# Value products of a sparse attention in one burst, compressed values last, probability tiles copied back in place

## The chip, the cores and the metric

One core of a Trainium2 chip runs the program. The time is that of the device, in microseconds, as the median of three runs. Below, PE is TensorE's matmul stream, PEld its weight loads, DVE is VectorE, ACT ScalarE, POOL GpSimd.

## What is computed

The reference is two layers of a decoder trunk over 512 tokens of width 1024. A layer's mixer sums three gated branches; the change touches one of them, the sparse attention with 8 heads in 2 groups (head width 64). For each query it adds three attentions over the same query, each weighted by a gate:

```
p_cmp = masked_softmax(s_cmp, cmp_mask)            # 31 compressed blocks of 32 tokens
o_cmp = einsum('bghsn,bngd->bsghd', p_cmp, vc)
...                                                 # selected blocks: all 8 of 64 tokens are taken at this length
p = masked_softmax(s, mask);  o_sel = einsum('bgqhn,bgqnd->bgqhd', p, vg)
...                                                 # window of 512 tokens: all earlier tokens
o_win = einsum('bnghqk,bnkgd->bnqghd', p_win, vw)
g = sigmoid(gate_logits)
o = g[..., 0:1] * o_cmp + g[..., 1:2] * o_sel + g[..., 2:3] * o_win
```

The other branches are two chunked linear recurrences. After the mixer come a cross attention over 256 memory tokens and a gated MLP with a short convolution.

## The kernel before

**Dense work.** Activations stand transposed (features on partitions, 512 tokens in a row). A weight arrives by DMA in pieces of 128 x 512, is split into a rounded part (ACT, into `wh`) and a rest (DVE, into `wl`), and each 128 x 128 piece is then used in three matmuls of 512 columns into one of three PSUM banks of the tag `pd`. There are three buffers for arriving weights and two for converted ones. Such dense matmuls (`fm_scaled` for the gates, `branch` for the branches' output weights) stand in the program before and after `nsa_attn`.

**The attention, `nsa_attn` (from line 1027).** The outer loop goes over four query blocks i of 128 tokens. Each makes the compressed scores and their probabilities for all heads, gated, transposed, in `pc`. The inner loop goes over four values of j, each a pair of heads, one of each group g_; this text calls such a pair a head. There are 16 heads per layer and 32 in all. For a head and each of 2 groups x 2 branches (br 0 selected, 1 window):

1. score matmuls (L1080 to L1082, 128 x (i+1) keys, into a `pa` bank), the maximum on DVE (L1084), the exponential on ACT into a tile `pr` of the tag `chain`, with its sum;
2. when all four are there: reciprocal, gate, and a scaling of the four `pr` (DVE, L250);
3. transposes of each `pr` in pieces of 128 (L1100, into a `pt` bank), and a copy of the bank by ACT into a new `chain` tile `pT`;
4. an output bank `po` of the tag `pa`: the compressed values (`vcpad`) times `pc` open the accumulation, two matmuls; then for each branch, each key block k and each group a value product `tok` x `pT`. Group 0 writes partitions 0 to 63, group 1 partitions 64 to 127;
5. a copy of the bank into the output `y` by ACT.

One fp32 product of step 4 shows as two instructions in the trace, so the compressed pair is x4 and the value products of a head in block i are x8(i+1). Transposes are x4(i+1).

**Buffers.** `chain` has 36 buffers, `pa` two banks, `pt` three.

**What sets the order.** The program's text gives each engine no fixed order. A planner goes through the instructions at build time, places on each engine what it takes to be ready, earliest in the program first (weight conversions ahead by a raised priority), gives out buffers as they come free, and sets a semaphore wait for each dependence on another engine. On the chip each engine's matmuls or operations then run in the order so fixed. Dense matmuls that stand in the program after the attention are thereby placed between its steps where these are not ready.

Of the kernel before, what the change touches and what calls it, by code (L numbers as in the profile page):

```python
# [13 lines left out]
AF = mybir.ActivationFunctionType  # L14
# [5 lines left out]
P = 128  # L20
# [179 lines left out]
def tile_trunk(ctx, tc, a, out, dbg=None):  # L200
    nc = tc.nc
    dbg = dbg or {}
    V, S, G, TE = nc.vector, nc.scalar, nc.gpsimd, nc.tensor
# [7 lines left out]
    def tl(tag, bufs, shape=(P, T), dt=F32):  # L211
        uid[0] += 1
        return sb.tile(list(shape), dt, tag=tag, name=f"{tag}_{uid[0]}", bufs=bufs)

    def chain():
        return tl("chain", NCHAIN)
# [5 lines left out]
    def pa():  # L222
        uid[0] += 1
        return pp.tile([P, T], F32, tag="pa", name=f"pa_{uid[0]}", bufs=2)

    def pt():
        uid[0] += 1
        return pp.tile([P, T], F32, tag="pt", name=f"pt_{uid[0]}", bufs=3)

    def small(n, dt=F32):  # L230
        if n <= 16:
            return tl("tiny", 40, (P, 16), dt)[:, :n]
        return tl("small", 10, (P, 64), dt)[:, :n]

    def mm(out_, lhsT, rhs, start=True, stop=True):
        TE.matmul(out_, lhsT, rhs, start=start, stop=stop, skip_group_check=True)  # L236
# [5 lines left out]
    def act(o, i, f=AF.Copy, **kw):  # L242
        S.activation(o, i, f, **kw)  # L243

    def tt(o, x, y, op, eng=None):
        (eng or V).tensor_tensor(o, x, y, op)  # L246

    def ts(o, x, s1, s2, op0, op1=None, eng=None):
        if op1 is None:
            (eng or V).tensor_scalar(o, x, s1, None, op0)  # L250
        else:
            (eng or V).tensor_scalar(o, x, s1, s2, op0, op1)
# [6 lines left out]
    def mark(name):  # L259
        if "mark" in dbg:  # L260
            dbg["mark"](name, nc)
# [193 lines left out]
    vcpad = [cst.tile([P, 4, 64], F32, name=f"vcpad{i}") for i in range(2)]  # L455
# [571 lines left out]
    def nsa_attn(l, tok, y, st):  # L1027
        KH, KL, QS, kcT, r8 = (st[k] for k in ("KH", "KL", "QS", "kcT", "r8"))
        mark("attn")
        gall = tl("gall", 1, (P, NT, 24))  # L1030
        act(gall, tok[:, :, TOK_G:TOK_G + 24], AF.Tanh, scale=0.5)
        ts(gall, gall, 0.5, 0.5, MUL, ADD)

        for i in range(NT):
            qs_ = slice(i * P, (i + 1) * P)
            sc = pa()
            for j in range(4):
                for g_ in range(2):
                    mm(sc[:, (4 * g_ + j) * 64:(4 * g_ + j + 1) * 64], QS[j, g_][:, qs_],
                       kcT[:, g_].rearrange("p a n -> p (a n)"))  # L1040
            e = tl("tg", NTG)[:, :256].rearrange("p (h n) -> p h n", h=8)
            m3 = cmpm[:, i:i + 1, :].to_broadcast([P, 8, 32])
            pen = tl("cmpn", 1, (P, 32))
            ts(pen, cmpm[:, i, :], -NEG, NEG, MUL, ADD)
            p3 = pen[:, None, :].to_broadcast([P, 8, 32])
            s4 = sc.rearrange("p (h a n) -> p h a n", a=2, n=32)
            tt(e, s4[:, :, 0], p3, ADD)
            tt(e, e, s4[:, :, 1], ADD)
            b8 = lambda t_, n_=32: t_.rearrange("p (h o) -> p h o", o=1).to_broadcast([P, 8, n_])
            tt(e, e, b8(r8[:, i]), MUL)  # L1050
            mx = small(8)
            V.tensor_reduce(mx, e, AX.X, MAX)
            tt(e, e, b8(mx), SUB)
            act(e, e, AF.Exp)
            tt(e, e, m3, MUL)
            dn = small(8)
            V.tensor_reduce(dn, e, AX.X, ADD)
            ts(dn, dn, 1e-30, None, MAX)
            V.reciprocal(dn, dn)
            g3 = gall[:, i, :].rearrange("p (h b) -> p h b", b=3)  # L1060
            cf = small(8)
            tt(cf, dn, g3[:, :, 0], MUL)
            tt(e, e, b8(cf), MUL)
            ps = pt()
            for g_ in range(2):
                TE.transpose(ps[:, g_ * P:(g_ + 1) * P], e[:, g_ * 4:g_ * 4 + 4, :].rearrange("p h n -> p (h n)"), ident)
            pc = tl("tg", NTG)
            act(pc[:, :256], ps[:, :256])

            for j in range(4):  # L1070
                hd = {}
                W = (i + 1) * P
                WM = max(W, 256)
                den = small(4)
                prs = []
                for g_ in range(2):
                    for br in range(2):
                        q_ = QS[j, g_][:, qs_]
                        ps = pa()
                        mm(ps[:, :WM], q_, KH[br, g_][:, :WM], stop=False)  # L1080
                        mm(ps[:, :WM], q_, KL[br, g_][:, :WM], start=False, stop=False)
                        mm(ps[:, i * P:W], identb, negb, start=False, stop=True)  # L1082
                        nm = small(1)
                        V.tensor_reduce(nm, ps[:, :W], AX.X, MAX, negate=True)  # L1084
                        rc = r8[:, i, 4 * g_ + j:4 * g_ + j + 1]
                        tt(nm, nm, rc, MUL)
                        pr = chain()
                        act(pr[:, :W], ps[:, :W], AF.Exp, bias=nm, scale=rc, accum_out=den[:, 2 * g_ + br:2 * g_ + br + 1])
                        prs.append(pr)
                V.reciprocal(den, den)  # L1090
                g4 = gall[:, i, :].rearrange("p (g j b) -> p g j b", g=2, b=3)[:, :, j, 1:]
                tt(den.rearrange("p (g b) -> p g b", g=2), den.rearrange("p (g b) -> p g b", g=2), g4, MUL)
                for g_ in range(2):
                    for br in range(2):
                        x_ = 2 * g_ + br
                        pr = prs[x_]
                        ts(pr[:, :W], pr[:, :W], den[:, x_:x_ + 1], None, MUL)
                        pst = pt()
                        for k in range(i + 1):
                            TE.transpose(pst[:, k * P:(k + 1) * P], pr[:, k * P:(k + 1) * P], ident)  # L1100
                        pT = chain()
                        act(pT[:, :W], pst[:, :W])
                        hd[g_, br] = pT
                po = pa()
                o_ = [po[g_ * 64:(g_ + 1) * 64, :P] for g_ in range(2)]
                for g_ in range(2):
                    mm(o_[g_], vcpad[g_][:, j, :], pc[:, g_ * P:(g_ + 1) * P], start=True, stop=False)
                for br, off in ((0, TOK_VS), (1, TOK_VW)):
                    for k in range(i + 1):
                        for g_ in range(2):  # L1110
                            mm(o_[g_], tok[:, k, off + g_ * 64:off + g_ * 64 + 64], hd[g_, br][:, k * P:(k + 1) * P],
                               start=False, stop=(br == 1 and k == i))
                act(y[j][:, qs_], po[:, :P])
                yield

# [92 lines left out]
    def mixer(l, norm):  # L1208
# [68 lines left out]
        for _ in nsa_attn(l, tok, ya, st):  # L1277
            pass
# [169 lines left out]
```

## Time and profile before

| | us |
|---|---|
| median of 3 runs | 2110.43 (2110.14 to 2110.9) |
| span of the profiled execution | 2108.7 |
| TensorE busy (matmuls) | 2057.5 |
| TensorE busy (weight loads) | 1610.2 |
| VectorE busy | 1430.0 |
| ScalarE busy | 951.3 |
| GpSimd busy | 131.9 |

The profiled execution's own time is its span and what lies around it before the first and after the last instruction; only the span is in the profile. Busy times are read against it. Matmuls overlap in the pipeline and their ends are modelled, so the distance from one start to the next tells what a matmul costs the stream, and its own duration doesn't. The two attention stretches are 372 to 554 us (layer 0) and 1405 to 1588 us (layer 1) from the span's start.

### The profile page before, as it was taken

What the parts mean: (1) busy time and instruction counts of PE and PEld (TensorE: products, weight loads), DVE (VectorE), ACT (ScalarE), POOL (GpSimd) and SP (SyncE); (2) the same over time, 40 slices, a digit from 0 to 9 for tenths busy, and PEclk for the clock granted to TensorE, in tenths of its full rate; (3) what the DMA queues carried; (4) which work ended last, traced back from release to release, by engine and by line L of the source; (5) the groups of instructions that cost most, each with busy time, mean ns of one, the idle gap of its engine ahead of it and who ended that gap; (6) DMA issues with size and microseconds to landing.
All of it is one profiled execution on the core that took longest, in us unless ns stands there. A gap on an engine that the chain in (4) does not pass through costs nothing. (4 is left out here: it accounts for less than half of the span.)

```text
span 2108.7 us, 31046 instructions
## 1 busy us (share of the span) xinstructions
PE 2057.5 (98%) x11396; PEld 1610.2 (76%) x11400; DVE 1430.0 (68%) x3070; ACT 951.3 (45%) x1854; POOL 131.9 (6%) x120
## 2 busy tenths in 40 slices
PE   8999999999999999999999998999999999999999
PEld 7877677777786788888888776777778758888887
DVE  6764898666656887377548469975667577755773
ACT  6434444555545544244434344445554454433442
POOL 1000122000010100000000003110000110000000
PEclk9999999999999999999999999999999999999999
DMA  7332222111241233323432312121113413333333
GB/s 237 90 101 68 77 74 64 52 51 46 64 140 47 88 95 95 95 94 96 120 107 76 101 42 90 59 72 51 46 46 91 126 52 92 95 93 98 95 98 108
DMA packets 116809, 180.90 MB, mean 86 GB/s; under 512 B 19696, under 2 KB 37232, under 8 KB 116656
## 3 DMA queue, kind: packets, MB, share of 16 engines
q1 hardware_dynamic: 88992, 158.64, 25.1%
q10 hardware_dynamic: 27584, 19.97, 3.3%
q8 instruction: 90, 1.47, 0.3%
q14 instruction: 63, 0.52, 0.1%
q0 software_dynamic: 80, 0.29, 0.0%
HBM read 170.21 MB, written 8.65 MB: 85 GB/s over the span
## 5 line engine op out<-in xcount | busy, mean ns | idle before, releaser
L236 PE MATMUL pd<-act,wh 128*128 128x512 f32 x3008 | 985.4, 403 | 0.0
L243 ACT ACTIVATE wh<-wr 128x512 fp32r<-128x512 f32 (+2 forms) x586 | 365.5, 624 | 657.5 <-PE pd L236 566.3
L236 PEld LDWEIGHTS pd<-act,wh 128*128 128x128 f32 x3008 | 560.6, 189 | 128.4 <-issue 14.4
L236 PE MATMUL pd<-act,wl 128*128 128x512 f32 x1504 | 605.6, 403 | 1.4 <-DVE wl L246 1.4
L246 DVE TENSOR_TENSOR wl<-wr,wh 128x512 fp32r<-128x512 f32 (+2 forms) x586 | 406.7, 694 | 212.3 <-ACT wh L243 205.0
L236 PE MATMUL pd<-chain,wh 128*128 128x512 f32 x1344 | 426.7, 397 | 4.4 <-DVE gate L255 3.2
L236 PEld LDWEIGHTS pd<-act,wl 128*128 128x128 f32 x1504 | 284.3, 189 | 69.0 <-issue 6.1
L236 PEld LDWEIGHTS pd<-chain,wh 128*128 128x128 f32 x1344 | 251.0, 188 | 66.0 <-ACT chain L243 3.7
L236 PE MATMUL pd<-chain,wl 128*128 128x512 f32 x672 | 266.4, 396 | 0.3
L246 DVE TENSOR_TENSOR gate<-pd,rb 128x512 f32<-128x512 f32 x168 | 116.0, 691 | 102.8 <-PE pd L236 101.3
L236 PE MATMUL pa<-chain,chain 128*64 128x64 f32 (+7 forms) x1248 | 163.2, 296 | 2.3 <-ACT chain L243 1.0
L236 PEld LDWEIGHTS pd<-chain,wl 128*128 128x128 f32 x672 | 126.6, 188 | 30.3 <-DVE wl L246 1.1
L255 DVE SCALAR_TENSOR_TENSOR gate<-gate,vec,gate 128x511 f32<-128x511 f32 (+1 forms) x176 | 132.1, 751 | 21.5 <-ACT gate L243 18.3
L236 PEld LDWEIGHTS pa<-chain,chain 128*64 128x64 f32 (+3 forms) x1248 | 109.1, 163 | 45.5 <-issue 21.0
L1084 DVE TENSOR_REDUCE tiny<-pa 128x1 f32<-128x128 f32 (+3 forms) x128 | 61.1, 487 | 81.7 <-PE pa L236 81.3
L243 ACT ACTIVATE chain<-pa,tiny,r 128x128 f32<-128x128 f32 (+3 forms) x128 | 78.9, 617 | 60.7 <-DVE tiny L246 56.3
L246 POOL TENSOR_TENSOR chain<-chain,t 128x512 f32<-128x512 f32 x30 | 40.7, 1355 | 1014.7 <-ACT t L243 949.0
L243 ACT ACTIVATE chain<-pt 128x512 f32<-128x512 f32 (+3 forms) x156 | 61.1, 445 | 63.9 <-PE pt L1100 37.2
L243 ACT ACTIVATE gate<-gate,vec 128x512 f32<-128x512 f32 x88 | 63.8, 726 | 27.9 <-DVE gate L246 27.9
L236 PE MATMUL pa<-chain,tok 128*64 128x128 f32 x704 | 62.3, 282 | 0.0
L255 DVE SCALAR_TENSOR_TENSOR t<-t,gate 128x512 f32<-128x512 f32 x88 | 60.5, 688 | 2.0 <-ACT t L243 0.4
L246 POOL TENSOR_TENSOR tg<-tg,chain 128x256 f32<-128x256 f32 (+1 forms) x42 | 45.5, 1089 | 191.1 <-ACT tg L243 78.5
(238 smaller groups left out, 2001.5 us busy)
## 6 DMA issues: line engine op xcount, KB each, us to landing
wr<-in_w_fm SPq DMA_DIRECT2D x184, 256.0 KB, 2.7
wr<-in_w_up SPq DMA_DIRECT2D x176, 256.0 KB, 2.6
wr<-in_w_dn SPq DMA_DIRECT2D x64, 256.0 KB, 2.7
wr<-in_w_mix SPq DMA_DIRECT2D x32, 256.0 KB, 2.7
wr<-in_w_dn SPq DMA_DIRECT2D x32, 192.0 KB, 2.4
wr<-in_w_tk SPq DMA_DIRECT2D x16, 272.0 KB, 2.9
wr<-in_w_kv SPq DMA_DIRECT2D x16, 256.0 KB, 3.8
chain<-in_cmp_w SPq DMA_DIRECT2D x16, 256.0 KB, 4.1
```

Source lines behind the costliest of these rows:

```text
L236: TE.matmul(out_, lhsT, rhs, start=start, stop=stop, skip_group_check=True)
L243: S.activation(o, i, f, **kw)
L246: (eng or V).tensor_tensor(o, x, y, op)
L255: V.scalar_tensor_tensor(o, x, s, y, op0, op1)
L1084: V.tensor_reduce(nm, ps[:, :W], AX.X, MAX, negate=True)
```

## The change

The copy out of the transposes' bank goes back into `pr` and not into a new tile. The first value product of each group (br 0, k 0) gets, besides its own dependences, one on the head's last copy, and opens the accumulation. The compressed products come last and close it. Nothing else in the program differs.

```diff
                         for k in range(i + 1):
                             TE.transpose(pst[:, k * P:(k + 1) * P], pr[:, k * P:(k + 1) * P], ident)
-                        pT = chain()
-                        act(pT[:, :W], pst[:, :W])
-                        hd[g_, br] = pT
+                        copied = S.activation(pr[:, :W], pst[:, :W], AF.Copy)
+                        hd[g_, br] = pr
                 po = pa()
                 o_ = [po[g_ * 64:(g_ + 1) * 64, :P] for g_ in range(2)]
-                for g_ in range(2):
-                    mm(o_[g_], vcpad[g_][:, j, :], pc[:, g_ * P:(g_ + 1) * P], start=True, stop=False)
                 for br, off in ((0, TOK_VS), (1, TOK_VW)):
                     for k in range(i + 1):
                         for g_ in range(2):
-                            mm(o_[g_], tok[:, k, off + g_ * 64:off + g_ * 64 + 64], hd[g_, br][:, k * P:(k + 1) * P],
-                               start=False, stop=(br == 1 and k == i))
+                            m_ = TE.matmul(o_[g_], tok[:, k, off + g_ * 64:off + g_ * 64 + 64],
+                                           hd[g_, br][:, k * P:(k + 1) * P],
+                                           start=(br == 0 and k == 0), stop=False, skip_group_check=True)
+                            if br == 0 and k == 0:
+                                tc.add_manual_dep(m_.ins, copied.ins.name, mybir.DependencyInfo(
+                                    mybir.DependencyClass.Sync, mybir.DependencyReason.DATA), reason="one burst")
+                for g_ in range(2):
+                    mm(o_[g_], vcpad[g_][:, j, :], pc[:, g_ * P:(g_ + 1) * P], start=False, stop=True)
                 act(y[j][:, qs_], po[:, :P])
```

## Rows read from the trace of the kernel before

**Rows 1.** The page, first part: busy us of each engine, share, instructions.
```profile
PE 2057.5 (98%) x11396; PEld 1610.2 (76%) x11400; DVE 1430.0 (68%) x3070; ACT 951.3 (45%) x1854; POOL 131.9 (6%) x120
```

**Rows 2.** Stretches: us, busy (count) of PE, PEld, DVE, ACT, POOL; clock, DMA, GB/s.
```profile
372.00:554.00 182.00, 182.00 (x1153) 133.83 (x1152) 112.72 (x326) 101.06 (x265) 0.00 (x0) 1.00 0.16 47
1405.00:1588.00 183.00, 182.93 (x1154) 134.02 (x1152) 113.25 (x327) 101.45 (x266) 0.00 (x0) 1.00 0.16 47
```

**Rows 3.** Waits: engine, line, waited for; us in total, times, longest.
```profile
PEld pa L236 <- issue: 52.0, 167, 3.1
```

**Rows 4.** Groups on PE, 372 to 554: count, busy us, mean ns, idle before.
```profile
L236 PE MATMUL pa<-chain,tok 128*64 128x128 f32 x320 | 27.2, 280 | 0.0
...
L236 PE MATMUL pa<-tg,vcpad 128*64 128x128 f32 x64 | 7.0, 298 | 0.0
```

**Rows 5.** Timeline of PE, first head of block 2: start, us, operation, count.
```profile
454.52 0.47 PE L236 MATMUL pd<-act,wl 128*128 128x512 f32 x1
454.92 0.44 PE L236 MATMUL pa<-tg,vcpad 128*64 128x128 f32 x4
455.29 0.72 PE L236 MATMUL pd<-chain,wh 128*128 128x512 f32 x2
455.85 0.62 PE L236 MATMUL pd<-act,wh 128*128 128x512 f32 x2
456.31 0.39 PE L236 MATMUL pd<-chain,wl 128*128 128x512 f32 x1
...
459.03 0.43 PE L236 MATMUL pa<-chain,tok 128*64 128x128 f32 x2
459.39 0.50 PE L236 MATMUL pd<-act,wh 128*128 128x512 f32 x1
459.82 1.52 PE L236 MATMUL pa<-chain,tok 128*64 128x128 f32 x22
461.28 0.62 PE L236 MATMUL pa<-chain,chain 128*128 128x384 f32 x2
461.74 0.23 PE L236 MATMUL pa<-negb,identb 128*128 128x128 bf16 x1
```

**Rows 6.** Timeline of PE: last head of block 1, and the next scores.
```profile
445.25 1.09 PE L236 MATMUL pa<-chain,tok 128*64 128x128 f32 x14
446.27 0.62 PE L236 MATMUL pa<-chain,chain 128*128 128x384 f32 x2
```

**Rows 7.** Timeline of PE: first product of the first and the last broken head.
```profile
393.75 0.43 PE L236 MATMUL pa<-chain,tok 128*64 128x128 f32 x2
...
1545.20 0.43 PE L236 MATMUL pa<-chain,tok 128*64 128x128 f32 x2
```

**Rows 8.** Timeline of ACT for the head of rows 5: probability copies, output copy.
```profile
458.01 1.64 ACT L243 ACTIVATE chain<-pt 128x384 f32<-128x384 f32 x4 [1.65 <-PE pt L1100]
...
461.38 0.28 ACT L243 ACTIVATE chain<-pa 128x128 f32<-128x128 f32 x1 [1.09 <-PE pa L236]
```

**Rows 9.** Timelines: the first head of block 0, the second of block 3.
```profile
378.32 0.95 ACT L243 ACTIVATE chain<-pt 128x128 f32<-128x128 f32 x4
378.89 0.87 PE L236 MATMUL pa<-chain,tok 128*64 128x128 f32 x8
379.69 0.50 PE L236 MATMUL pd<-act,wl 128*128 128x512 f32 x1
...
524.83 2.06 ACT L243 ACTIVATE chain<-pt 128x512 f32<-128x512 f32 x4 [2.68 <-PE pt L1100]
526.07 2.35 PE L236 MATMUL pa<-chain,tok 128*64 128x128 f32 x32
528.35 0.73 PE L236 MATMUL pa<-chain,chain 128*128 128x512 f32 x2
```

**Rows 10.** Timeline behind layer 0's attention: last output split, first branch product.
```profile
555.87 0.68 DVE L246 TENSOR_TENSOR chain<-chain,chain 128x512 fp32r<-128x512 f32 x1
...
560.00 0.62 PE L236 MATMUL pd<-chain,wh 128*128 128x512 f32 x2
```

## The prediction

> **What bounds the kernel now.** I read the page first, then the stretches, the waits, the groups and last the order on TensorE. TensorE is busy for 2057.5 of 2108.7 us, VectorE for 68% [rows 1]. In the two stretches in which the attention runs, TensorE is busy all the time at a granted clock of 1.00, that is the 2.4 GHz level, while ScalarE and VectorE are busy for 55 and 62% [rows 2]. So only work or lost slots on TensorE can shorten these stretches, or work that runs out beside them.
>
> The Trainium skill (Perfetto Trace Analysis, "Identifying the Most-Contended Engine") warns that matmul busy time is a bad measure of what is left, since matmuls are pipelined; the next row bears that out. The weight loads ahead of matmuls into `pa` stand idle for 52.0 us in 167 places, and no other engine is named [rows 3]: the array is between two kinds of matmul. The value products (320 in one stretch) and the compressed products (64) use 64 columns of the array, the dense ones all 128 [rows 4].
>
> **What a break costs** is read from starts in TensorE's order, in the first head of the third query block [rows 5]. Dense matmuls follow each other every 0.23 us (two from 455.85 to 456.31). Ahead of the compressed products a dense one takes 454.52 to 454.92 = 0.40, and the products take 0.37 until the next dense one: 0.77, of which 0.23 is the dense matmul's own. So this little group costs 0.54 us. Later the value products come in two pieces: one product (x2) takes 0.36, a single dense one 0.43 (0.20 over its own), the other eleven (x22) 1.46 until the next scores. A run of x14 takes 1.02 [rows 6]; eight instructions more, two pairs of both head groups, cost 0.44, so a pair inside a run takes 0.22. The compressed pair stands 0.37, so leaving a run costs 0.15, and the lone product 0.36 - 0.15 = 0.21, as much as a pair: it has no partner in the other half of the array.
>
> **The change, part by part.**
> 1. Compressed products last. Per head 0.54 goes and one more pair at the end of the burst, 0.22, comes: 0.32 x 32 heads = **10.2 us**. The output copy by ScalarE follows that pair, and next to nothing else waits for it. No DMA is issued by what moves, and no queue but TensorE's is passed.
> 2. One burst. A product in two pieces costs 0.36 + 0.43 - 0.23 + 1.46 = 2.02 us; six pairs and one exit cost 6 x 0.22 + 0.15 = 1.47. Gain 0.55 per broken head. Through both stretches 20 of the 32 heads are broken (the first and the last in [rows 7]), 18 times by one dense matmul, else by transposes: 20 x 0.55 = **11.0 us**.
> 3. The added wait. The first products wait for the fourth copy, not the first. In the head of [rows 5] the copies end at 458.01 + 1.64 = 459.65, 0.62 us after the products began [rows 8]. In a first block it is 0.38 (379.27 against 378.89), in a last block 0.82 (526.89 against 526.07) [rows 9]; the second block is put between, at 0.50 (an estimate from its neighbours). All heads: 8 x (0.38 + 0.50 + 0.62 + 0.82) = 18.6 us. Queued behind the waiting matmul are TensorE's own: the rest of the burst, the next scores, dense matmuls. In a broken head a dense matmul was ready to stand in the gap, so I take the wait as covered there by dense matmuls drawn forward, which have to be run anyway. Going from transposes to a dense one and then into the burst (0.20) replaces going from transposes straight into it, which I put at zero, within 0.2 either way. In the 12 unbroken heads (four of the first block, two of the second, six of the last) nothing ready stood between; uncovered it is 4 x 0.38 + 2 x 0.50 + 6 x 0.82 = 7.4 us. Against that, these heads wait inside the burst now: x32 should take 8 x 0.22 + 0.15 = 1.91 and takes 2.28 (528.35 - 526.07), x8 should take 0.59 and takes 0.80 (379.69 - 378.89). This goes: 6 x 0.37 + 4 x 0.2, and 2 x 0.2 with the second block taken like the first, = 3.4. Net between -3.4 (covered) and +4.0 us; I take **+1**, a little on the uncovered side: the x32 head, the longest of these waits, found no dense matmul before, though a longer gap leaves it more time to.
> 4. Copies in place. The four ScalarE copies stay as long (1.64 us for four), and read the same transposes they waited for already. Four of the 36 `chain` buffers per head are not taken. The waits view names none for a free buffer, so I count 0. A gain is not excluded (to -2, an allowance without a row); a loss I exclude, since a head now takes four buffers where it took eight.
> 5. The output bank. Now one of two `pa` banks is taken at 454.92 by the compressed products and freed by the output copy at 461.38 + 0.28 = 461.66 [rows 5, 8]: 6.7 us. Then its first writer comes after the copies, at 459.65. If the planner hands out the bank only with that first write, the next head's scores get it nearly 5 us sooner and heads overlap more; if it keeps it from the turn of the output tile in the program, nothing changes. The trace before can't tell. TensorE has no idle time to win there, so I count 0 in the sum, but it decides the rivals.
>
> Sum: -10.2 - 11.0 + 1 = -20.2 us. The profiled span is 2108.7; the median of the runs is 2110.4, 1.7 us more, which lies around the span and stays. 2110.4 - 20.2 = **2090 us**.
>
> The Trainium skill (TensorE: Matmul & The Clock Gate, "Part 3: Packing small matmuls") says that a weight load overlaps running matmuls only where its row group differs. Both halves here use all rows, so by that page a product gains nothing from a partner. The two lone ones of a broken head (the first, and the one left over of eleven) would then cost no more than in pairs, part 2 would lose one slot of 0.22 per broken head, 20 x 0.22 = 4.4 us, and the time would be 2094. The row of x22 against x14 shows a pair in 0.22 where one alone takes 0.21, so the trace does not agree, and the sum stays.
>
> **Rivals.**
> - *Heads overlap more.* With the bank free early, scores run ahead, every wait for the copies is covered (another 4.4 us) and the pairs of scores that queue just behind a burst (0.46 from 461.28 to 461.74 [rows 5], where two of 384 columns at the dense 0.23 per 512 would take 0.35) lose some 0.1 us each, in 32 heads to twice as often. 2090 - 4.4 - 5 (of 3 to 6) = 2081. For it: the bank is held 6.7 us, a burst needs it for 2. Against: the scores may need VectorE and ScalarE first.
> - *The attention's own chain sets the stretch.* If the bank is kept, a head's chain (scores, exponential, transposes, copies, burst, output copy, next scores) ends where the burst ends. By the row sums the new end is 459.65 + 7 x 0.22 + 0.15 = 461.34 against 461.28, but in an unbroken last-block head 526.89 + 9 x 0.22 + 0.15 = 529.02 against 528.35, +0.67. Summed with the other blocks in the same way the chain grows some 4 to 6 us a layer, while TensorE's work falls by 10. The dense work beside the attention is nearly used up at its end: the last split of its output ends at 555.87 + 0.68 = 556.55, and the branch product that needs it starts at 560.00 [rows 10], so 3.4 us are left, and matmuls of the branch that don't need the last output can run ahead: with two buffers of converted weights, nine of twelve matmuls each, 18 x 0.23 = 4.2 us more. Then the gain is 3.4 to 7.6 minus 5 per layer, from +1.6 lost to 2.6 gained: 2105 to 2113, no change.
> - *Slower: the last copy comes late.* In that same case a weight conversion (0.63 us on ScalarE, taken ahead by its priority) lands between the copies. If half the heads get one, the chain grows by 16 x 0.63 = 10 and 5 us more per layer; less 3.4 to 7.6 of cover that is 7 to 12 us per layer: about 2125 to 2134. It decides from a growth of some 0.34 us per head (the mean cover of 5.5 us over 16 heads). For it: all waits become one, at the head of an in-order queue. Against: four copies now run within 1.64 us unbroken [rows 8].
> - *Only half of it happens.* Dense matmuls of higher priority still break the burst, and only part 1 pays, 2100. The dependence makes all products ready at once, which speaks against it.
>
> **How the numbers follow.** The forecast (2084 to 2095) 0.50; half of it (2095 to 2105) 0.20; more overlap (below 2084) 0.13; the chain sets the stretch (2105 to 2113) 0.10; slower 0.07. Outside 0.2%, or 4.2 us, which is about what a measurement of this kernel can tell from no change, lies all of the first three and a part of the fourth: faster 0.84, same 0.09, slower 0.07. To hold 8 in 10 the range takes the first two whole, the overlap case down to 2079 (its 2081 and the 2 us of part 4) and the fourth to 2107: 2079 to 2107.
>
> **What would show it.** Right: in TensorE's order no compressed products ahead of the transposes, one run of value products per head with the compressed pair at its end, the idle time of weight loads before `pa` matmuls down by some 15 us or more, dense matmuls between transposes and burst. The x22 row becomes x24 without a break. The two stretches should each be about 10 us shorter with TensorE still busy throughout. Wrong: TensorE idle before the burst with ScalarE named, or idle after the last head ahead of the branch products (the chain); or bursts in pieces (half of it). The planner orders the whole program anew, so other stretches may move by a few us, which I have no row for; if they move by 10, the forecast fails for a reason outside these steps.

## The result, and the profile after

The changed kernel takes 2137.26 us (2135.89 to 2141.9, four runs) against 2110.28 in runs of the kernel before beside it: ratio 1.0132 [1.0119, 1.0144]. It is **slower by 27 us**, where 20 us less was forecast.

First the busy times, which answer to [rows 1].

```profile
PE 2050.4 (96%) x11396; PEld 1614.0 (76%) x11400; DVE 1433.6 (67%) x3070; ACT 957.4 (45%) x1854; POOL 133.2 (6%) x120
```

The span is 2136.5 us. TensorE was idle for 2108.7 - 2057.5 = 51.2 us before and for 2136.5 - 2050.4 = 86.1 us now: 34.9 more, while its busy time fell by 7.1; 34.9 - 7.1 = 27.8 is the longer span. Where the idle time lies is read from windows. The rows have the columns of [rows 2].

```profile
456.00:512.00 56.00, 56.00 (x364) 43.09 (x363) 38.07 (x95) 29.76 (x70) 0.00 (x0) 1.00 0.19 59
512.00:528.00 16.00, 15.61 (x79) 11.58 (x76) 12.53 (x33) 7.69 (x17) 0.00 (x0) 1.00 0.16 50
528.00:576.00 48.00, 34.28 (x251) 26.79 (x249) 19.37 (x50) 22.56 (x49) 0.00 (x0) 0.82 0.05 12
1560.00:1624.00 64.00, 44.81 (x312) 34.40 (x306) 31.09 (x79) 29.76 (x63) 0.00 (x0) 0.89 0.06 17
```

Up to 528 us the attention of layer 0 shows TensorE busy (but for 0.4 us) at a clock of 1.00, as before [rows 2]. Then 13.7 of 48 us are idle and the clock falls; in the second layer 19.2 of 64. In the kernel before the same two windows have 0.2 us of idle time each:

```profile
528.00:576.00 48.00, 47.77 (x275) 36.89 (x272) 32.03 (x64) 24.30 (x49) 0.00 (x0) 1.00 0.22 61
1560.00:1624.00 64.00, 63.77 (x362) 50.17 (x361) 43.90 (x81) 32.44 (x63) 0.00 (x0) 1.00 0.22 67
```

So 32.4 of the 34.9 us lie in these two windows, at the **end of each layer's attention**, and not in the blocks ahead of it, whose heads have the edit's wait as well. The next view is the dense matmuls (tile `pd`) of the changed kernel alone: us, busy (count), clock.

```profile
512.00:530.00 18.00, 13.66 (x50) 1.00 0.19 59
530.00:576.00 46.00, 2.42 (x8) 0.81 0.03 6
```

The dense work beside the attention is used up at 530 us, and the attention goes on nearly alone until its last value product at 575.33; before, that product stood at 552.36, with dense matmuls beside it to the end. So the attention ends 23 us later and has lost its cover. Why it became longer is seen where TensorE still is busy: the second head of block 2, in TensorE's order (the columns of [rows 5]).

```profile
473.81 0.62 PE L236 MATMUL pa<-chain,chain 128*128 128x384 f32 x2
...
474.31 0.59 PE L236 MATMUL pa<-chain,chain 128*128 128x384 f32 x2
...
476.71 0.54 PE L236 MATMUL pa<-chain,chain 128*128 128x384 f32 x2
...
478.84 0.61 PE L236 MATMUL pa<-chain,chain 128*128 128x384 f32 x2
...
482.67 0.49 PE L1100 MATMUL pt<-cm,chain 128*128 128x128 f32 x3
...
484.15 1.14 PE L1100 MATMUL pt<-cm,chain 128*128 128x128 f32 x9
...
485.98 1.53 PE L1108 MATMUL pa<-chain,tok 128*64 128x128 f32 x24
487.34 0.39 PE L236 MATMUL pa<-tg,vcpad 128*64 128x128 f32 x4
487.66 0.61 PE L236 MATMUL pa<-chain,chain 128*128 128x384 f32 x2
```

The burst is what was wanted: twelve products without a break in 487.34 - 485.98 = 1.36 us, the compressed pair behind them in 0.32. But all four score groups of a head stand **behind the burst** of the head ahead of it (473.81 to 478.84), and none of the next head's comes before its transposes and burst are through (487.66). In the kernel before, one group ran ahead. The same head there; the burst and the score group right behind it, at 461.28, are in [rows 5]:

```profile
456.77 0.51 PE L236 MATMUL pa<-chain,chain 128*128 128x384 f32 x2
...
461.78 0.60 PE L236 MATMUL pa<-chain,chain 128*128 128x384 f32 x2
...
464.20 0.51 PE L236 MATMUL pa<-chain,chain 128*128 128x384 f32 x2
...
465.47 0.44 PE L236 MATMUL pa<-tg,vcpad 128*64 128x128 f32 x4
...
468.03 0.51 PE L236 MATMUL pa<-chain,chain 128*128 128x384 f32 x2
...
469.66 0.49 PE L1100 MATMUL pt<-cm,chain 128*128 128x128 f32 x3
```

Only three groups of this head follow the burst (461.28, 461.78, 464.20); a fourth had been there ahead of it, at 456.77. The compressed products take the output's bank at 465.47, and a score group of the *next* head stands at 468.03, ahead of the transposes. So its maximum and exponential pass while the head ahead of it is still being transposed.

**The theory.** The two `pa` banks are given to the tiles in the order of the program. The output tile `po` stands there ahead of the next head's scores. Before, its first writer (the compressed products) needs nothing of this head, so it claims its bank at once, and the tile behind it, the next scores, gets the other. After, its first writer waits for the last copy, so the claim comes late, and **the tiles behind it wait too, though a bank is free**. The head loses its overlap, the attention grows, its cover of dense work ends too soon. The planner's hand-out itself is in no trace, but what it leaves on the chip is. In the changed kernel's second head of block 2, ScalarE reads the last of the four score groups out of its bank until 480.78 + 0.67 = 481.45:

```profile
480.78 0.67 ACT L243 ACTIVATE chain<-pa,tiny,r 128x384 f32<-128x384 f32 x1 [0.83 <-DVE tiny L246]
```

The burst writes its bank from 485.98 on. For the 4.5 us between, TensorE's order has no matmul into either `pa` bank. Dense matmuls and this head's transposes fill that time; the next head's scores, which need nothing of this head, don't stand there. In all 32 heads of the changed kernel the order is four score groups, transposes, burst, compressed pair. In the kernel before, a score group of the next head stands between compressed products and transposes in 24 heads, all but the last of each block; there, in six of eight, it is the next block's compressed scores.

The rivals: the added wait itself, the copies in place, or a cost on TensorE of the new accumulation order.

### The profile page after: what moved, and what is told of

It reads as the page before. It is cut to its first block, busy times and chain, and to the rows that moved or that the text cites. A ratio compares the mean times of both kernels' runs of the same rounds, so it can differ in the third digit from the quotient of the medians.

```text
span 2136.5 us, 31148 instructions
## 1 busy us (share of the span) xinstructions
PE 2050.4 (96%) x11396; PEld 1614.0 (76%) x11400; DVE 1433.6 (67%) x3070; ACT 957.4 (45%) x1854; POOL 133.2 (6%) x120
## 4 chain that ended last, share of the span: by engine, by line
PE 85%; DVE 9%; ACT 2%; issue 2%; DMA 1%; DVEq 0%; ACTq 0%; POOLq 0%
PE pd L236 67%; PE pa L236 11%; PE pt L1100 2%; PE pa L1108 2%; DVE wl L246 2%; DVE chain L246 2%; DVE gate L246 1%; ACT chain L243 1%; DVE tg L246 1%; PE pt L236 1%; DMA wr<-in_w_kv 1%; PE pt L430 1%; DVE gate L255 0%; DVE tiny L1084 0%; DVE act L255 0%
## 5 line engine op out<-in xcount | busy, mean ns | idle before, releaser
L255 DVE SCALAR_TENSOR_TENSOR gate<-gate,vec,gate 128x511 f32<-128x511 f32 (+1 forms) x176 | 132.1, 751 | 21.3 <-ACT gate L243 18.2
L1100 PE MATMUL pt<-cm,chain 128*128 128x128 f32 x320 | 58.4, 327 | 14.6 <-DVE chain L250 14.4
L1101 ACT ACTIVATE chain<-pt 128x128 f32<-128x128 f32 (+3 forms) x128 | 51.0, 437 | 43.2 <-PE pt L1100 27.9
L1100 PEld LDWEIGHTS pt<-cm,chain 128*128 128x128 f32 x320 | 46.4, 169 | 28.2 <-DVE chain L250 21.8
```

Of the source, the lines that this page charges most:

```text
L255: V.scalar_tensor_tensor(o, x, s, y, op0, op1)
L1101: copied = S.activation(pr[:, :W], pst[:, :W], AF.Copy)
```

## The experiments

**e1_in_place.** The kernel before, with the copies in place alone.

```diff
-                        pT = chain()
-                        act(pT[:, :W], pst[:, :W])
-                        hd[g_, br] = pT
+                        act(pr[:, :W], pst[:, :W])
+                        hd[g_, br] = pr
```

> The kernel before with one part of the change alone: the probability copy goes back into its own tile. Three theories of the 27 us. Bank: the pa banks are handed out in the order of the program, and the output tile, whose first matmul now stands behind the copies, holds up the next head's first scores. Wait: the burst's wait for the last copy lengthens each head. In place: the probability tiles are held longer, through the burst. Bank and wait: no change, 2107 to 2114 us. In place: most of the loss, 2125 to 2137.

2108.56 us against 2110.61, ratio 0.9994 [0.9983, 1.0005]: nothing. The copies neither cost nor bring a measurable time; 22 of the 32 heads are still in pieces (20 before).

**e2_first_and_burst.** The change, with the compressed products back at the front; the added wait stays.

```diff
+                for g_ in range(2):
+                    mm(o_[g_], vcpad[g_][:, j, :], pc[:, g_ * P:(g_ + 1) * P], start=True, stop=False)
...
-                                           start=(br == 0 and k == 0), stop=False, skip_group_check=True)
+                                           start=False, stop=(br == 1 and k == i), skip_group_check=True)
...
-                for g_ in range(2):
-                    mm(o_[g_], vcpad[g_][:, j, :], pc[:, g_ * P:(g_ + 1) * P], start=False, stop=True)
```

> The changed kernel with the compressed products back in front, opening the accumulation; the value products still wait for the last copy, copies still in place. Bank: the output's bank is claimed early again, one score group of the next head runs ahead of the transposes, 11 us of the burst are saved and the chain grows by the wait alone: 2098 to 2112 us, TensorE idle in the last block only a little. Wait: still slow, 2125 to 2140. In place: still slow, 2125 to 2140.

2095.97 us, ratio 0.9928 [0.9910, 0.9946]: 14.6 us faster than before. The wait for the last copy is in this kernel and costs it nothing that shows, so it isn't the cause of the loss. In its order a score group stands ahead of the transposes again:

```profile
455.91 0.44 PE L236 MATMUL pa<-tg,vcpad 128*64 128x128 f32 x4
...
456.84 0.51 PE L236 MATMUL pa<-chain,chain 128*128 128x384 f32 x2
...
459.17 1.62 PE L1100 MATMUL pt<-cm,chain 128*128 128x128 f32 x12
...
461.42 1.53 PE L1110 MATMUL pa<-chain,tok 128*64 128x128 f32 x24
```

**e3_last_no_wait.** The change without the added dependence.

```diff
-                            if br == 0 and k == 0:
-                                tc.add_manual_dep(m_.ins, copied.ins.name, mybir.DependencyInfo(
-                                    mybir.DependencyClass.Sync, mybir.DependencyReason.DATA), reason="one burst")
```

> The changed kernel without the added dependence: compressed products last, copies in place, each value product waits only for its own copy. Bank: the output's bank is claimed by the first value product, still behind the transposes, so no score runs ahead: slow, 2120 to 2137 us, with TensorE idle in the last block of each layer. Wait: the compressed products' 10 us are gained, 2098 to 2106. In place: 2125 to 2140.

2134.5 us, ratio 1.0112 [1.0088, 1.0137]. Without the wait the loss is still there: compressed products last are enough for it. The first products now wait for the first copy instead of the last, which still is late. In many heads a score matmul of the next head stands right behind that first product, which fits the theory: it comes as soon as the output has claimed its bank.

```profile
481.60 0.43 PE L1108 MATMUL pa<-chain,tok 128*64 128x128 f32 x2
481.96 0.44 PE L236 MATMUL pa<-chain,chain 128*128 128x384 f32 x1
482.34 1.42 PE L1108 MATMUL pa<-chain,tok 128*64 128x128 f32 x21
```

**e4_own_bank and e4b_before_own_bank.** The output tile gets a bank of its own (the transposes give one up); the first in the changed kernel, the second in the kernel before, so that the price of the banks is known by itself.

```diff
-        return pp.tile([P, T], F32, tag="pt", name=f"pt_{uid[0]}", bufs=3)
+        return pp.tile([P, T], F32, tag="pt", name=f"pt_{uid[0]}", bufs=2)
...
-                po = pa()
+                uid[0] += 1
+                po = pp.tile([P, T], F32, tag="po", name=f"po_{uid[0]}", bufs=1)
```

> The changed kernel with a PSUM bank of its own for the attention's output, taken from the transposes (two in place of three); everything else as in the change. Bank: the next heads' scores run ahead of the transposes by two or three groups, TensorE no longer idle in the last block, the 21 us of the burst come through less what the missing transpose bank costs: 2085 to 2103 us. Wait or in place: still slow, 2125 to 2140.

> The kernel before with the output bank of its own (two transpose banks, not three), and nothing of the change. It tells how much of the 25.7 us that the changed kernel with its own bank gained is the bank's and how much the change's. If the change's TensorE savings (10 from the compressed products, 11 from the burst) come through only now: 2102 to 2112 us here. If the bank alone makes the gain: 2085 to 2095.

e4: 2084.86 us, ratio 0.9881 [0.9863, 0.9899]. e4b: 2117.66 us, ratio 1.0040 [1.0028, 1.0053]. The new banks alone cost 7 to 9 us; with them the change is worth 2117.66 - 2084.86 = 33 us. Nothing but the banks was altered in e4, so, with e2, the late claim in a *shared* set of banks carries the loss; no extra cost of the accumulation order on TensorE is left.

**e5_scores_ahead.** The two shared banks as in the change, but the next head's first score group is written into the program ahead of the output tile, inside a block. For that the score group became a function, `score`; only the lines that call it ahead are shown.

```diff
...
+                if j < 3:
+                    den_ = small(4)
+                    ahead = den_, [score(j + 1, 0, den_)]
                 po = pa()
```

> The changed kernel, with the next head's first score group written in the program ahead of the output tile (within a block; not from one block to the next). PSUM banks as in the change. Hand-out in the order of the program: the first scores get their bank before the output tile stands in line, heads overlap by one group as before the change, and the savings come through: 2088 to 2106 us. If the bank were held, or two banks too few for the burst, whatever the order in the program: 2125 to 2140.

2138.15 us, ratio 1.0138 [1.0123, 1.0153]: a **miss**, 2088 to 2106 had been expected. The place of a head's last value product in layer 0, us from the span's start, tells how far it came:

| us | before | after | e5 |
|---|---|---|---|
| last head of block 1 | 446.07 | 455.18 | 447.23 |
| first head of block 2 | 461.07 | 473.39 | 467.97 |
| last head of block 2 | 496.92 | 511.72 | 505.00 |
| first head of block 3 | 514.26 | 531.80 | 528.14 |
| last head of block 3 | 552.36 | 575.33 | 576.04 |

Inside the first blocks most of the loss is taken back. But at the change of block, where the old order was left, e5 falls behind: 447.23 to 467.97 is 20.7 us against 15.0 before, and 505.00 to 528.14 is 23.1 against 17.3. In the kernel before, the next block's compressed scores, whose tile is of the tag `pa` too, ran ahead there (those of block 2 from 442.05, four us before the last product of block 1). In e5, as in after, they stand behind the last head's burst (those of block 3 from 505.42). With 13.9 us lost by 528 us e5 also meets the end of the dense work, and there it loses what it was ahead of after:

```profile
505.00:528.10 23.10, 23.10 (x145) 17.87 (x143) 16.09 (x39) 11.23 (x24) 0.00 (x0) 1.00 0.19 58
528.10:576.00 47.90, 32.51 (x201) 25.28 (x199) 17.54 (x46) 19.82 (x42) 0.00 (x0) 0.68 0.02 6
```

TensorE is idle for 15.4 of the last 47.9 us, at a clock of 0.68 where after has 0.82: more of its work is done at half the clock. Why its crossings take 2.5 and 3.1 us more than those of after (18.2 and 20.1) stays open.

**e7_ahead_across.** e5, and at the last head of a block the next block's compressed scores and first score group are written ahead of the output tile as well. Banks as in the change. The diff is against e5; the compressed scores became a function, `compressed`.

```diff
...
-                if j < 3:
+                n_ = 4 * i + j + 1
+                if n_ < 4 * NT:
+                    if n_ % 4 == 0:
+                        pcs[n_ // 4] = compressed(n_ // 4)
                     den_ = small(4)
-                    ahead = den_, [score(j + 1, 0, den_)]
+                    ahead = den_, [score(n_ // 4, n_ % 4, 0, den_)]
```

> As the run with the first scores written ahead of the output tile, and the same from block to block: the next block's compressed scores and its first score group also stand in the program ahead of the last head's output tile. That run kept the heads' distance of before within a block (13.2, 11.6, 12.3 us in block 2) and lost it between blocks (17 to 23 us against 15 to 17). If the hand-out in program order is the cause, the distances between blocks return as well: 2090 to 2108 us, TensorE not idle in the last block by more than 2 us per layer. If something else in the change lengthens the chain: 2120 to 2138.

2089.13 us, ratio 0.9904 [0.9888, 0.9921]. The order of the tiles alone takes back 48 us from after. The crossings into blocks 2 and 3 now take 13.8 and 14.3 us, and the layer's last value product stands at 549.61. Its order in block 2, and the window to the end of layer 0's attention:

```profile
458.33 1.53 PE L1124 MATMUL pa<-chain,tok 128*64 128x128 f32 x24
459.69 0.39 PE L236 MATMUL pa<-tg,vcpad 128*64 128x128 f32 x4
460.01 0.62 PE L236 MATMUL pa<-chain,chain 128*128 128x384 f32 x2
...
460.51 0.59 PE L236 MATMUL pa<-chain,chain 128*128 128x384 f32 x2
...
463.38 0.58 PE L236 MATMUL pa<-chain,chain 128*128 128x384 f32 x2
...
464.16 0.51 PE L236 MATMUL pa<-chain,chain 128*128 128x384 f32 x2
...
467.18 0.49 PE L1110 MATMUL pt<-cm,chain 128*128 128x128 f32 x3
```

```profile
498.00:550.00 52.00, 51.80 (x362) 38.79 (x360) 33.14 (x78) 30.68 (x66) 0.00 (x0) 1.00 0.17 52
```

Three of the four groups behind the burst belong to this head, the fourth (464.16) to the next one. TensorE is busy to the end at full clock.

**e6_more_cover and e6b_before_more_cover.** Is it the lost cover that makes the longer chain cost time? Both kernels get 72 dense matmuls per layer behind the attention whose result nobody reads.

```diff
+        for n in range(3):
+            fm_proj(norm, w_fm(l, f"mb{n}"))
```

> The changed kernel with 72 dense matmuls more per layer, put behind the attention in the program, whose results nothing reads: at 0.23 us each 16.7 us per layer, 33.4 in all. If the loss is dense work that ran out beside a longer chain of heads, these fall into the idle and half-clock time of the last block: 2135 to 2150 us, hardly slower than the changed kernel (2137). If the time was lost otherwise: 2165 to 2172.

> The kernel before with the same 72 dense matmuls more per layer, as the price of the addition where TensorE is not idle: 2110 + 33 = 2140 to 2148 us by either theory.

In the kernel before the extra work costs 38 us (2146.63 against 2108.82, ratio 1.0177 [1.0153, 1.0200]). In the changed one it costs nothing: 2134.72 (1.012 [1.010, 1.014]) against 2137.26 without. So the time at the attention's end was empty enough to take it whole, and with this cover in both the change is 2146.63 - 2134.72 = 12 us *faster* than the kernel before. The window of after's idle time, in the changed kernel with this cover:

```profile
528.00:576.00 48.00, 43.93 (x311) 33.12 (x311) 26.23 (x60) 25.13 (x54) 0.00 (x0) 0.93 0.14 39
```

It is not filled whole (43.93 of 48 us, clock 0.93), which fits 12 us and not the 20 forecast.

**e8_own_bank_no_wait.** e4 without the added dependence (the diff of e3): what the burst is worth once the bank is out of the way.

> The changed kernel with an output bank of its own, without the added dependence on the last copy. With the chain out of the way it prices the burst alone: value products are in pieces again, and if these cost what the rows of before said (0.55 us for each of some 20 broken heads) the time is some 8 to 12 us more than the 2084.9 of the run with the dependence: 2092 to 2098 us. If the wait costs as much as the burst saves: 2082 to 2088.

2105.05 us, ratio 0.9971 [0.9962, 0.9980]: the burst is worth 2105.05 - 2084.86 = 20.2 us. Other work stands between the products in 28 of the 32 heads, in none of e4's. One of these:

```profile
463.69 0.43 PE L1109 MATMUL po<-chain,tok 128*64 128x128 f32 x2
464.06 0.50 PE L236 MATMUL pd<-act,wh 128*128 128x512 f32 x1
464.39 0.33 PE L236 MATMUL pa<-chain,chain 128*128 128x384 f32 x1
464.66 1.42 PE L1109 MATMUL po<-chain,tok 128*64 128x128 f32 x21
```

The prediction's price of 0.55 us a head gives 28 x 0.55 = 15.4 us; here two visitors stand in the gap, and some heads are in three pieces.

## Why the prediction was wrong, point by point

1. **Compressed products last (10.2 us).** On TensorE as forecast: the group's 0.54 us ahead of the transposes are gone, the pair at the burst's end takes 487.66 - 487.34 = 0.32 where 0.22 + 0.15 = 0.37 was put for it with the exit. No run does this part alone in the two shared banks. With a bank of its own for the output, e8 against e4b does it (the copies in place, which e1 priced at nothing, differ too): 2117.66 - 2105.05 = 12.6 us. In the shared banks e7 is 6.8 us faster than e2, which lacks it, but the two also differ in order.
2. **One burst (11.0 us).** Right in kind: none of 32 heads is broken. In size it was too low: e8 against e4 gives 20.2 us for 28 heads, 0.72 each where 0.55 was put. One dense matmul alone stands in the gap of 16 of the 20 heads, not 18; in the other four (401.38 and 494.55 in layer 0, 1434.79 and 1527.95 in layer 1) there are transposes as well, and two of the 16 have a second gap with transposes in it. The weight loads' idle time ahead of `pa` was to fall by 15 us or more. The row of [rows 3] falls from 52.0 to 40.2, but the value products now have a row of their own, in which ScalarE is named:

```profile
PEld pa L236 <- issue: 40.2, 136, 3.1
...
PEld pa L1108 <- ACT chain L1101: 15.3, 32, 1.1
```

   ScalarE's name ahead of the burst was to be a sign of being wrong, yet e7, which gains, has such a row too (11.7 us, 32 times). This sign did not tell the two cases apart. Parts 2 to 4 were put at -10; e2, which does these three, gave -14.6. The size was somewhat low.
3. **The added wait (+1).** Right that it is covered while dense work lasts: e2 keeps it and gains, e3 drops it and is still slow. Where the dense work has run out, TensorE does stand idle for it, 0.69 us in the head at 543.79 (the last view below).
4. **Copies in place (0).** Right (e1).
5. **The output bank (0).** *This step failed.* It named two outcomes: the bank is handed out with its first write and the next scores get it sooner, or it is kept from the turn of the tile in the program and nothing changes. The runs show a third one: handed out late, and until then no later tile of the tag gets any bank. The account of the planner ahead of the prediction, by which buffers are given out as they come free, lacks this order. I looked at how long *one* bank is held, and not at who stands in line behind the claim. That the moved products open a claim that had cost nothing was to be seen in [rows 5]: they stand 459.03 - 454.92 = 4.1 us ahead of the first value product. A score group of the next head stands between, at 456.77, in the part that I left out of those rows.
6. **The rival with the chain** named the right place ("idle after the last head ahead of branch products") and the right point of decision, the dense work that is left, but its growth was mis-sized: 4 to 6 us a layer, from the burst's end alone. The last value product of layer 0 moved by 575.33 - 552.36 = 23.0 us, 1.4 per head, since a score group with its reduction and exponential went back into the chain. Of this 14.8 us were there at the end of block 2, before any idle time; the slower clock has a part in the rest. This is the chain of waits in one uncovered head (us, engine, tile, line):

```profile
534.04 0.88 ACT chain L243 x2
...
534.96 0.82 PE pa L236 x3
...
539.43 3.69 PE pt L1100 x16
...
543.79 3.68 PE pa L1108 x32
```

   The second pair of scores (534.96) starts when the first pair's exponentials have emptied the banks (534.04 + 0.88 = 534.92). In the trace before, one of the four groups was through before the burst.
7. **The slower rival** took the wait for the last copy for the cause. With that wait e2 gains, and without it e3 is still slow, so it does not carry the loss. That this rival had the sign and nearly the size (2125 to 2134) is luck.
8. **The rule on weight loads.** The Trainium skill (TensorE: Matmul & The Clock Gate, "Part 3: Packing small matmuls") says that a weight load overlaps running matmuls only where its row group differs. That a product therefore gains nothing from a partner (a sum of 2094) was the prediction's own step; the page does not say so, and its table in the same section has a gain for tiles that differ in their columns. The burst agrees with a gain: twelve products in 1.36 us are 0.113 each, half of a lone one's 0.21.

So the forecast 2090 comes out where the overlap is kept: 2089.13 in e7. That the total agrees is partly luck. In the shared banks parts 2 to 4 came to 14.6 us (e2) where 10 had been put, and the rest to 6.8 (e7 against e2) where part 1 was put at 10.2; with a bank for the output they are 20.2 and 12.6. What failed is the claim that the rest of the schedule stays as it is.

## What to carry to other kernels

When the first writer of a buffer is moved, ask not only how long the buffer is held, but which tiles of the same set are handed out behind it: here a late first write, with a second bank free, kept the next head's scores back and turned what is 21 us of gain in e7 into 27 of loss. Two repairs work, a bank of its own for the late tile (2084.9), or writing the work that should run ahead ahead of it in the program, across every loop boundary (2089.1; within the inner loop alone it brought nothing). And before trusting a saving on a full engine, measure how much independent work is left at the end of the stretch: a saving uses it up sooner, and a longer chain shows only then.

## What was not expected of the hardware

In the windows of after in which TensorE has idle time, part of what is left on it is slower as well. Seven stretches stand at half the clock, the 1.2 GHz level. The longest and the sum of all seven, with the columns of [rows 2]:

```profile
538.70:548.90 10.20, 8.78 (x55) 7.53 (x56) 1.83 (x5) 2.67 (x5) 0.00 (x0) 0.50 0.00 0
...
sum 30.60, PE 28.37 PEld 26.47 DVE 9.95 ACT 12.50 POOL 0.00; mean PE 4.05 PEld 3.78 DVE 1.42 ACT 1.79 POOL 0.00
```

They hold 28.4 us of busy time, of which about half, 14 us, is due to the clock (an estimate: at full clock the same work would take half as long, as the x32 below does). That is most of why TensorE's busy time fell by 7.1 us only, where in e7, which has as many instructions, it fell by 24.3, from 2057.5 to 2033.2. In order, 2.87 us of idle time lie just ahead of the work in the first of them; a burst of x32 takes 3.47 us to the compressed pair there, and 1.79 in the same kernel one head earlier:

```profile
530.11 1.97 PE L1108 MATMUL pa<-chain,tok 128*64 128x128 f32 x32
531.90 0.39 PE L236 MATMUL pa<-tg,vcpad 128*64 128x128 f32 x4
...
539.43 3.68 PE L1100 MATMUL pt<-cm,chain 128*128 128x128 f32 x16 [2.87 <-DVE chain L250]
543.79 3.68 PE L1108 MATMUL pa<-chain,tok 128*64 128x128 f32 x32 [0.69 <-ACT chain L1101]
547.26 0.64 PE L236 MATMUL pa<-tg,vcpad 128*64 128x128 f32 x4
```

The prediction priced lost cover as idle time alone; the granted clock added to it.
